# Fewer lone convolution taps on VectorE, two more whole weight tiles, and a norm's first sums written later, in a fused two-block kernel

## The chip, the cores and the metric

The kernel runs on one core of a Trainium2 chip. The metric is device time in microseconds (us) of one execution. All times below are of that core: TensorE (PE, and PEld for its weight loads), VectorE (DVE), ScalarE (ACT), GpSimd (POOL) and SyncE (SP, which issues the weight transfers).

## What is computed

Two model blocks in a row on 256 tokens of width 1024, all in fp32. The first block (retention, then latent attention) is not touched. The change lies in the first half of the second block:

```python
h = layer_norm(x) * (1.0 + sc1[:, None]) + sh1[:, None]
proj = h @ w_in[l]
a_val, a_gate, u_pool, gate_a, gate_b = jnp.split(proj, [COL_A_VAL, COL_A_GATE, COL_POOL, COL_GATE_A], axis=-1)

ya = a_val * jax.nn.sigmoid(a_gate)                     # 512 channels
ya = causal_dwconv(ya, w_dw_a[l], b_dw_a[l])            # 31 taps per channel
ya = jax.nn.silu(layer_norm(ya, ln_a_g[l], ln_a_b[l]))
ya = ya @ w_pw_a[l]

pooled = causal_multiscale_pool(u_pool)                 # windows 2, 4, 8, 16
yb = jnp.einsum("bsgc,gcd->bsgd", pooled, w_pool[l]).reshape(bsz, s, D_MODEL) * pool_scale[l]
merged = jax.nn.sigmoid(gate_a) * ya + jax.nn.sigmoid(gate_b) * yb
mix = merged @ w_out[l]
```

## The kernel before

Activations lie channels by tokens: a block is 128 channels by 256 tokens, and four blocks fill one buffer of the pool `half`, which has 14 buffers. A product in fp32 is done in one of two ways. `mm` (lines 237 to 239) takes weight and activation split into a high and a low part and makes three products; for that each weight tile of 128x1024 goes through a cast on ScalarE (`wh`, line 178) and a subtraction on VectorE (`wl`, line 179). `mm32` (line 243) takes both whole, in one fp32 instruction that runs four passes, and needs neither step. `in_tile(ps, m, parts)` picks one of the two for one tile of 128 output channels of `w_in2`.

The stretch that the change touches runs on TensorE in this order: four tiles ahead of the norm (`ahead_mm`), four tiles `[2, 6, 3, 7]` (`k_outer`), four tiles of the pool's input and two of a gate by `mm32`, then fourteen tiles of the gates by `mm` in seven pairs, with the eight small products of `w_pool` after the third pair, then `w_pw` (`half_outer`), which needs the convolution's norm `yap`.

Beside it run these steps.

- `modulate` (line 993 and on) makes the norm's output `h` per block: the high part on ScalarE (L993), the full value on VectorE (L995; kept as `hraw` in two buffers of `half` for the `mm32` tiles), the low part on VectorE (L996).
- `conv_steps` does the 31 taps for two channel blocks at a time, first half blocks 0 and 1, second half blocks 2 and 3. A step is either a **double step** (0 in `STEPS`): ScalarE scales two taps for two blocks into a fresh buffer `t` of `half` (four instructions, L1105) and VectorE adds the 128x1024 of it to the accumulator (L1106); or a **lone tap** (1): two fused multiply-adds on VectorE (L1099). The last addition of a half is L1109. `every(1.35, ...)` writes one step each 1.35 us of planned TensorE time.
- `pool(g)`, four groups: GpSimd adds shifted copies (L1165, in two buffers `lv`), VectorE finishes (L1167, L1169, L1170, buffer `pq`), and `split` makes the two parts for `w_pool` (L187, L188).
- `ln_a_first` squares the first half's result and sums both on TensorE (L1180, L1185); `ln_a` does so for the second half (L1190, L1193), and then computes the statistics, the scale, the SiLU (L1201) and its split (L187, L188), which `w_pw` waits for.

What is written where comes from a small planner in the code: `tick` counts planned TensorE time, and `after(us, fn)` and `every` write a step when its time has come. A scheduler then orders each engine's queue from that and gives each new tile a buffer; a buffer that is still held is a wait. Each engine works its queue strictly in order.

Of the kernel before, what the change touches and what calls it, by code (L numbers as in the profile page):

```python
# [14 lines left out]
AF = mybir.ActivationFunctionType  # L15
ALU = mybir.AluOpType
ADD, SUB, MUL = ALU.add, ALU.subtract, ALU.mult
# [65 lines left out]
def tile_kernel(ctx, tc, order, xT, pT, pos, vec, cst, cv, rows, wada, wts, outT):  # L83
    nc = tc.nc
    V, A, T = nc.vector, nc.scalar, nc.tensor
# [11 lines left out]
    def nm(s):  # L97
        uid[0] += 1
        return f"{s}_{uid[0]}"
# [4 lines left out]
    def bank2():  # L104
        return bank().rearrange("p (b t) -> p b t", b=2)
# [28 lines left out]
    def t2(dt=F32):  # L134
        return tp.tile([P, 2, S], dt, tag="t2", name=nm("t2"), bufs=6)
# [46 lines left out]
    def nouter(name, ms, kbs, c0=0):  # L182
        return [(name, kb * P, c0 + m * P) for m in ms for kb in kbs]
# [19 lines left out]
    def after(us, fn):  # L203
        queue.append((clk[0] + us, fn))
        queue.sort(key=lambda e: e[0])
# [79 lines left out]
    def col(name, i, n=1):  # L285
        o = VOFF[name] + i
        return vc[:, o:o + n]
# [110 lines left out]
    def bc2(t, n=2):  # L398
        return t.unsqueeze(1).to_broadcast([P, n, S])
# [25 lines left out]
    def every(us, n, step):  # L425

        def run():
            step()
            if n > 1:
                every(us, n - 1, step)  # L430
        after(us, run)
# [379 lines left out]
    for i in range(3):  # L811
        ps = bank2()
# [170 lines left out]
    def modulate(x, which, mu, nrl, pairs, pair, raw=None):  # L983

        shift = mod[:, 24 * which:24 * which + 8]
        for i in pairs:
            t = t2()
            V.tensor_sub(t, x.pair(i), bc2(mu))
            V.tensor_mul(t, t, bc2(nrl))
            for b in range(2):  # L990
                k = 2 * i + b
                m1 = ms[:, 8 * which + k:8 * which + k + 1]
                A.activation(pair[0][k], t[:, b, :], AF.Identity, bias=shift[:, k:k + 1], scale=m1)  # L993
                full = t[:, b, :] if raw is None else raw[k]
                V.tensor_scalar(full, t[:, b, :], m1, shift[:, k:k + 1], MUL, ADD)  # L995
                V.tensor_sub(pair[1][k], full, pair[0][k].bitcast(F32))  # L996


# [78 lines left out]
    def tap(i, k):  # L1077
        return apad[:, i, k:k + S], col("w_dw_a_2", 4 * k + i)


    STEPS = [0, 0, 1, 0, 0, 1, 0, 1, 0, 1, 0, 1, 0, 1, 0, 0, 1, 0]

    def conv_steps():
        for i0 in (0, 2):
            own = acc2[i0 // 2]
            for k in range(2):
                for b in range(2):
                    x, w = tap(i0 + b, k)
                    if k == 0:
                        A.activation(own[:, k, b, :], x, AF.Identity, bias=col("b_dw_a_2", i0 + b), scale=w)  # L1090
                    else:
                        A.activation(own[:, k, b, :], x, AF.Copy, scale=w)
            yield
            k = 2
            for i, alone in enumerate(STEPS):
                if alone:
                    for b in range(2):
                        x, w = tap(i0 + b, k)
                        V.scalar_tensor_tensor(own[:, 0, b, :], x, w, own[:, 0, b, :], MUL, ADD)  # L1099
                else:  # L1100
                    t = hp_.tile([P, 2, 2, S], F32, tag="half", name=nm("half"))
                    for j in range(2):
                        for b in range(2):
                            x, w = tap(i0 + b, k + j)
                            A.activation(t[:, j, b, :], x, AF.Copy, scale=w)  # L1105
                    V.tensor_add(own, own, t)  # L1106
                k += 1 if alone else 2
                if i == len(STEPS) - 1:
                    V.tensor_add(own[:, 0], own[:, 0], own[:, 1])  # L1109
                    if i0 == 2:  # L1110
                        after(0.6, ln_a)
                if i0 == 2 and i == 1:
                    ln_a_first()
                yield
            assert k == 31
# [17 lines left out]
    glu_ahead(0)  # L1133
    modulate(xt, 0, mu, nrl, range(2, 4), hp, hraw)
    glu_ahead(1)
    every(1.35, 2 + 2 * len(STEPS), conv)
    pab = k_outer("w_in2", [2, 6, 3, 7], hp)
    for i in (2, 3):
        glu(pab[i - 2], i)
# [4 lines left out]
    def in_tile(ps, m, parts):  # L1144
        seq = Seq(nouter("w_in2", [m], range(8)), parts=parts)
        for kb in range(8):
            if parts:
                mm(ps, seq.next(), rhs(hp, kb), kb == 0, kb == 7)
            else:
                mm32(ps, seq.next()[0], hraw[kb], kb == 0, kb == 7)  # L1150

    for i in range(2):
        ps = bank2()
# [66 lines left out]
    for i in range(8):  # L1220
        j = (i + 4) % 8
        ps = bank2()
        for b in range(2):
            in_tile(ps[:, b, :], 12 + 2 * j + b, i > 0)
        A.activation(sab.pair(j), ps, AF.Sigmoid)
        if i == 3:
            pool_out()
# [145 lines left out]
    for i in range(NA + 2, FB):  # L1373
        ps = bank2()
# [15 lines left out]
    ps = {(tb, o): bank()[:, :w] for tb in range(2) for o, w in chunks[tb]}  # L1390
# [27 lines left out]
    for tb in range(2):  # L1418
# [3 lines left out]
        for o, w in chunks[tb]:  # L1422
# [5 lines left out]
            t = zt[o // 512][:, o % 512:o % 512 + w]  # L1428
# [96 lines left out]
```

## Time and profile before

| | us |
|---|---|
| median of 3 runs | 862.32 (860.01 to 863.61) |
| the profiled execution | 856.09 |
| its span from first to last instruction | 854.2 |
| PE busy in the span | 826.4 (97%) |
| DVE busy | 713.1 (83%) |
| ACT busy | 551.4 (65%) |
| POOL busy | 21.6 (3%) |

The profiled execution is 1.89 us longer than its span, and 6.23 us below the median of the runs. Busy shares are averages over the whole program. Matmuls overlap each other, so the duration of one is longer than its spacing to the next; in a row "x4" with one duration, that duration is from the start of the first to the end of the last.

### The profile page before, as it was taken

The numbers are of one execution on the slowest core, as the hardware profiler recorded it, in microseconds if no ns is written. First come the engines' busy times: TensorE is split into PE (matmuls) and PEld (weight loads), VectorE is DVE, ScalarE is ACT, GpSimd is POOL, SyncE is SP. The second block draws the span as 40 slices with busy tenths as digits, with TensorE's granted clock in tenths as the row PEclk, the third lists the DMA queues.
The fourth block names the chain that finished last, engine by engine and source line by source line (L and its number), as shares of the span: only waits on it lengthen the run. The fifth ranks groups of instructions, "written<-read, shape, count | busy, mean of one in ns | idle before, by whom it ended". The sixth has DMA issues, their size and how long they took to land.

```text
span 854.2 us, 15883 instructions
## 1 busy us (share of the span) xinstructions
PE 826.4 (97%) x6178; PEld 790.3 (93%) x6178; DVE 713.1 (83%) x1276; ACT 551.4 (65%) x950; POOL 21.6 (3%) x40
## 2 busy tenths in 40 slices
PE   9999999999999999998999999989799999999995
PEld 6989999999999899998999999889699999999885
DVE  6999788988898978688864868999777888889986
ACT  7656555555675786777754767888656576666550
POOL 0000000000000000000000000310000000000001
PEclk9999999999999999999999999999899999999998
DMA  9876567788466546364345354245453355557822
GB/s 336 317 264 217 206 216 256 260 286 324 153 204 236 203 156 249 141 221 148 128 166 189 123 178 170 98 145 197 143 206 123 127 196 178 192 205 255 275 79 74
DMA packets 46635, 167.49 MB, mean 196 GB/s; under 512 B 5216, under 2 KB 5472, under 8 KB 46560
## 3 DMA queue, kind: packets, MB, share of 16 engines
q1 hardware_dynamic: 45936, 164.38, 54.2%
q0 software_dynamic: 624, 2.10, 0.8%
q8 instruction: 48, 0.79, 0.4%
q14 instruction: 27, 0.22, 0.1%
HBM read 165.41 MB, written 1.05 MB: 195 GB/s over the span
## 4 chain that ended last, share of the span: by engine, by line
PE 43%; DVE 7%; ACT 3%; issue 1%; POOL 0%; DVEq 0%; ACTq 0%
PE ps L238 13%; PE ps L239 12%; PE ps L237 12%; PE ps L243 4%; DVE half L1106 2%; ACT half L1105 1%; DVE wl L179 1%; PE ps L343 1%; DVE half L1099 1%; POOL lv L1165 0%; PE ps L365 0%; DVE half L1218 0%; PE ps L922 0%; ACT half L993 0%; DVE t L1452 0%
## 5 line engine op out<-in xcount | busy, mean ns | idle before, releaser
L237 PE MATMUL ps<-half,wh 128*128 128x256 f32 x1568 | 443.5, 284 | 7.0 <-ACT half L187 7.0
L238 PE MATMUL ps<-half,wh 128*128 128x256 f32 x1568 | 444.3, 283 | 0.8 <-DVE half L188 0.8
L239 PE MATMUL ps<-half,wl 128*128 128x256 f32 x1568 | 440.8, 281 | 2.0 <-DVE wl L179 2.0
L178 ACT CAST wh<-raw 128x1024 fp32r<-128x1024 f32 x241 | 251.2, 1049 | 165.5 <-PE ps L238 105.0
L179 DVE TENSOR_TENSOR wl<-raw,wh 128x1024 fp32r<-128x1024 f32 x241 | 292.8, 1221 | 62.7 <-ACT wh L178 60.8
L237 PEld LDWEIGHTS ps<-half,wh 128*128 128x128 f32 x1568 | 295.6, 189 | 8.1 <-ACT half L187 7.6
L239 PEld LDWEIGHTS ps<-half,wl 128*128 128x128 f32 x1568 | 296.6, 189 | 2.6 <-DVE wl L179 2.6
L238 PEld LDWEIGHTS ps<-half,wh 128*128 128x128 f32 x1568 | 296.2, 189 | 2.3 <-DVE half L188 1.4
L237 PE MATMUL ps<-wh,half 128*128 128x512 f32 (+1 forms) x202 | 72.8, 361 | 0.0
L238 PE MATMUL ps<-wl,half 128*128 128x512 f32 (+1 forms) x202 | 71.1, 352 | 0.0
L415 DVE CUSTOM_DVE_ANT_0 adach<-adach,siluc 128x1024 f32<-128x1024 f32 x48 | 58.4, 1218 | 15.2 <-DMA adach<-in_wada 14.9
L239 PE MATMUL ps<-wh,half 128*128 128x512 f32 (+1 forms) x202 | 71.0, 351 | 0.0
L243 PE MATMUL ps<-half,raw 128*128 128x260 f32 (+2 forms) x256 | 56.7, 381 | 0.0
L243 PEld LDWEIGHTS ps<-half,raw 128*128 128x128 f32 x256 | 48.4, 190 | 6.9
L237 PEld LDWEIGHTS ps<-wh,half 128*128 128x128 f32 x202 | 38.1, 188 | 5.5 <-issue 0.5
L239 PEld LDWEIGHTS ps<-wh,half 128*128 128x128 f32 x202 | 38.0, 188 | 5.6
L238 PEld LDWEIGHTS ps<-wl,half 128*128 128x128 f32 x202 | 38.1, 189 | 5.4 <-DVE wl L179 0.4
L1105 ACT ACTIVATE half<-apad,vec 128x256 f32<-128x256 f32 x88 | 37.2, 502 | 2.9 <-DVE half L1106 2.9
L187 ACT CAST half<-t 128x256 fp32r<-128x256 f32 (+1 forms) x47 | 20.6, 453 | 17.8 <-DVE t L1365 10.8
L1106 DVE TENSOR_TENSOR half<-half,half 128x1024 f32<-128x1024 f32 x22 | 27.5, 1250 | 2.5 <-ACT half L1105 1.9
L188 DVE TENSOR_TENSOR half<-t,half 128x256 fp32r<-128x256 f32 (+1 forms) x47 | 21.7, 483 | 4.5 <-ACT half L187 3.6
L1360 ACT ACTIVATE t<-ps,vec 128x256 f32<-128x256 f32 x38 | 21.0, 558 | 2.0 <-PE ps L239 1.3
(294 smaller groups left out, 925.8 us busy)
## 6 DMA issues: line engine op xcount, KB each, us to landing
raw<-in_wts SPq DMA_DIRECT2D x257, 512.0 KB, 4.1
adach<-in_wada SPq DMA_DIRECT2D x48, 512.0 KB, 4.9
half<-in_xT SPq DMA_DIRECT2D x4, 256.0 KB, 6.3
half<-in_rows POOLq DMA_DIRECT2D x2, 512.0 KB, 4.7
out<-t SPq DMA_DIRECT2D x4, 256.0 KB, 2.0
cst<-in_cst SPq DMA_DIRECT2D x1, 928.0 KB, 10.3
raw<-in_wts SPq DMA_DIRECT2D x2, 256.0 KB, 4.3
siluc<-in_cv SPq DMA_DIRECT2D x1, 512.0 KB, 8.1
```

The costliest lines, as they stand in the source:

```text
L178: A.copy(hi, raw)
L179: V.tensor_sub(lo, raw, hi.bitcast(F32))
L187: A.copy(hi, src)
L188: V.tensor_sub(lo, src, hi.bitcast(F32))
L237: T.matmul(ps, l[0], r[0], start=first, stop=False)
L238: T.matmul(ps, l[0], r[1], start=False, stop=False)
L239: T.matmul(ps, l[1], r[0], start=False, stop=last)
L243: T.matmul(ps, w, r, start=first, stop=last)
L415: V.tensor_tensor_reduce(ch, ch, sc, 1.0, 0.0, MUL, ADD, mod[:, n:n + 1])
L1105: A.activation(t[:, j, b, :], x, AF.Copy, scale=w)
L1106: V.tensor_add(own, own, t)
L1360: A.activation(t[:, b, :], ps[:, b, :], AF.Identity, bias=col("b_dw_f_2", m), scale=w[2])
```

## The change

Four edits, all in the second block's first half. (1) `modulate`: where the full value is kept as `hraw` (the first of its two uses), it is computed by ScalarE, not VectorE. (2) `STEPS`: per half three lone taps and thirteen double steps instead of seven and eleven, and the period of writing is 1.5 instead of 1.35 us. (3) The first sums of the norm are written after the fifth step of the second half, not after the second. (4) `in_tile(..., i % 4 > 0)`: the pair `i = 4` is done whole, by `mm32`, too; the pair `i = 0` already was.

```diff
                 full = t[:, b, :] if raw is None else raw[k]
-                V.tensor_scalar(full, t[:, b, :], m1, shift[:, k:k + 1], MUL, ADD)
+                if raw is None:
+                    V.tensor_scalar(full, t[:, b, :], m1, shift[:, k:k + 1], MUL, ADD)
+                else:
+                    A.activation(full, t[:, b, :], AF.Identity, bias=shift[:, k:k + 1], scale=m1)
                 V.tensor_sub(pair[1][k], full, pair[0][k].bitcast(F32))
...
-    STEPS = [0, 0, 1, 0, 0, 1, 0, 1, 0, 1, 0, 1, 0, 1, 0, 0, 1, 0]
+    STEPS = [0, 0, 0, 0, 1, 0, 0, 0, 0, 1, 0, 0, 0, 0, 1, 0]
...
-                if i0 == 2 and i == 1:
+                if i0 == 2 and i == 4:
                     ln_a_first()
...
-    every(1.35, 2 + 2 * len(STEPS), conv)
+    every(1.5, 2 + 2 * len(STEPS), conv)
...
-            in_tile(ps[:, b, :], 12 + 2 * j + b, i > 0)
+            in_tile(ps[:, b, :], 12 + 2 * j + b, i % 4 > 0)
```

The edits shift the lines behind them by three: L1099, L1105, L1106, L1109 become L1102, L1108, L1109, L1112, and L1185, L1193, L1201 become L1188, L1196, L1204. The order of the queues is the same as before up to the second block's first norm, and again from `w_pw` on. Three places show what moved between.

ScalarE around the start of the convolution's second half, before (`half<-apad` scales a tap, `wh<-raw` casts a weight tile, `half<-ps` is a gate's sigmoid, `half_6775<-half_6772` splits a pooled group):

```order
L1105 ACTIVATE half_6841<-apad,vec 128x256 x4
L1090 ACTIVATE half_6485<-apad,vec 128x256 [waits DVE_49]
L1090 ACTIVATE half_6485<-apad,vec 128x256
L1092 ACTIVATE half_6485<-apad,vec 128x256 x2
L1105 ACTIVATE half_6900<-apad,vec 128x256 x4
L1105 ACTIVATE half_6929<-apad,vec 128x256 [waits DVE_49]
L1225 ACTIVATE half_6779<-ps_6828 128x512 [waits PE_49]
L1105 ACTIVATE half_6929<-apad,vec 128x256 x3
L1180 ACTIVATE t_1233_6937<-half_6484 128x512 [waits DVE_49]
L1105 ACTIVATE half_6981<-apad,vec 128x256 [waits DVE_49]
L1105 ACTIVATE half_6981<-apad,vec 128x256 x3
L187 CAST half_6775<-half_6772 128x256
```

The same place after the change, from the last two of five weight casts and the split of the last pooled group on (the second half's first taps, L1093 and L1095, stand eleven rows above):

```order
L178 CAST wh_7079<-raw_7077 128x1024 [waits DMAHW5_49]
L178 CAST wh_7117<-raw_7115 128x1024 [waits DMAHW6_49]
L187 CAST half_6787<-half_6784 128x256 [waits DVE_49]
L1108 ACTIVATE half_6862<-apad,vec 128x256 [waits DVE_49]
L1108 ACTIVATE half_6862<-apad,vec 128x256 x3
L178 CAST wh_7227<-raw_7225 128x1024 [waits DMAHW0_49,PE_49]
L1108 ACTIVATE half_6889<-apad,vec 128x256 [waits DVE_49]
L1108 ACTIVATE half_6889<-apad,vec 128x256 x3
L178 CAST wh_7302<-raw_7300 128x1024 [waits DMAHW1_49,PE_49]
L1108 ACTIVATE half_6922<-apad,vec 128x256 [waits DVE_49]
L1108 ACTIVATE half_6922<-apad,vec 128x256 x3
```

Before, the double steps of the second half follow at once on its first taps and go on between the pooled groups. Now none stands ahead of the last pooled group's split; the first of them waits for VectorE's side of that split (it takes the buffer `pq`), and each of the next three waits for VectorE's addition of the one before.

TensorE at the last pair of gate tiles, before, from the pair's last product on:

```order
L239 MATMUL ps_7425<-half_6459,wl_7459 128x256
L1193 MATMUL ps_6935<-half_6485,ones 128x256 [waits DVE_49]
L1193 MATMUL ps_6935<-half_6485,ones 128x256
L1193 MATMUL ps_6936<-t_1290_7371,ones 128x256 [waits Activation_49]
L1193 MATMUL ps_6936<-t_1290_7371,ones 128x256
L237 MATMUL ps_7491<-half_6773,wh_7495 128x256 [waits Activation_49]
```

And after, from the pair's first product on:

```order
L237 MATMUL ps_7393<-half_6458,wh_7396 128x256 [waits PE_49,Activation_49]
L238 MATMUL ps_7393<-half_6460,wh_7396 128x256
L239 MATMUL ps_7393<-half_6458,wl_7397 128x256 [waits DVE_49]
L237 MATMUL ps_7393<-half_6458,wh_7396 128x256
L238 MATMUL ps_7393<-half_6460,wh_7396 128x256
L239 MATMUL ps_7393<-half_6458,wl_7397 128x256
L237 MATMUL ps_7393<-half_6458,wh_7396 128x256
L1196 MATMUL ps_6974<-half_6485,ones 128x256 [waits DVE_49]
```

The norm's last sums stood behind the 48 matmuls of the last pair; now they stand behind seven of them, and 41 follow.

ScalarE in the norm, before, from the square of the second half to the SiLU:

```order
L178 CAST wh_7669<-raw_7667 128x1024 [waits DMAHW3_49,DVE_49,PE_49]
L1190 ACTIVATE t_1290_7371<-half_6485 128x512 [waits DVE_49]
L389 ACTIVATE t_1291_7377<-ps_6935 128x256 [waits PE_49]
L391 ACTIVATE t_1292_7379<-ps_6935 128x256
L395 ACT_TABLE_LOAD
L395 ACTIVATE t_1294_7383<-t_1293_7381,eps_l 128x256 [waits DVE_49]
L1201 ACT_TABLE_LOAD
L1201 ACTIVATE t_1298_7391<-t_1298_7391,vec,lng 128x256 [waits DVE_49]
```

And after:

```order
L1193 ACTIVATE t_1280_7256<-half_6485 128x512 [waits DVE_49]
L389 ACTIVATE t_1281_7262<-ps_6974 128x256 [waits PE_49]
L391 ACTIVATE t_1282_7264<-ps_6974 128x256
L178 CAST wh_7534<-raw_7532 128x1024 [waits DMAHW1_49]
L395 ACT_TABLE_LOAD
L395 ACTIVATE t_1284_7268<-t_1283_7266,eps_l 128x256 [waits DVE_49]
L178 CAST wh_7570<-raw_7568 128x1024 [waits DMAHW2_49,PE_49,Activation_49]
L178 CAST wh_7637<-raw_7635 128x1024 [waits DMAHW3_49,PE_49,Activation_49]
L1204 ACT_TABLE_LOAD
L1204 ACTIVATE t_1288_7276<-t_1288_7276,vec,lng 128x256 [waits DVE_49]
```

Three weight casts that stood ahead of the norm now stand inside it, the last of them (it takes the buffer of the last gate tile's weights, and waits for TensorE to be done with them) right ahead of the SiLU; on VectorE four of their subtractions stand inside the norm in the same way.

## Rows read from the trace of the kernel before

**Rows 1.** The page's first part: busy us, share of the span, instructions.

```profile
PE 826.4 (97%) x6178; PEld 790.3 (93%) x6178; DVE 713.1 (83%) x1276; ACT 551.4 (65%) x950; POOL 21.6 (3%) x40
```

**Rows 2.** Whom PE waited for, 500 to 620: us in total, times, longest.

```profile
PE ps L237 <- ACT half L187: 5.3, 1, 5.3
PE ps L1185 <- DVE half L1109: 2.3, 1, 2.3
PE ps L239 <- DVE wl L179: 1.1, 1, 1.1
PE ps L1193 <- DVE half L1109: 0.7, 1, 0.7
```

**Rows 3.** Stretches: length, busy us of PE, PEld, DVE, ACT, POOL; clock; DMA.

```profile
580.00:590.00 10.00, 8.91 (x75) 8.71 (x74) 10.00 (x16) 10.00 (x19) 0.00 (x0) 1.00 0.49 162
590.00:600.00 10.00, 10.00 (x87) 10.00 (x86) 10.00 (x13) 6.50 (x10) 0.00 (x0) 1.00 0.72 249
600.00:610.00 10.00, 3.98 (x25) 3.19 (x23) 9.04 (x14) 6.91 (x12) 0.00 (x0) 0.87 0.68 223
...
612.00:614.00 2.00, 2.00 (x11) 2.00 (x11) 0.17 (x1) 1.99 (x3) 0.00 (x0) 0.50 0.00 0
614.00:616.00 2.00, 2.00 (x18) 2.00 (x16) 0.06 (x1) 1.14 (x2) 0.00 (x0) 0.93 0.03 8
```

**Rows 4.** Timeline of PE: start, us, instructions, [idle before and releaser].

```profile
532.83 20.88 PE L243 MATMUL ps<-half,raw 128*128 128x256 f32 x96
553.36 0.47 PE L237 MATMUL ps<-half,wh 128*128 128x256 f32 x1
...
560.50 0.28 PE L239 MATMUL ps<-half,wl 128*128 128x256 f32 x1
...
564.46 1.13 PE L1185 MATMUL ps<-half,ones 128*128 128x256 f32 x4 [2.26 <-DVE half L1109]
...
609.84 0.79 PE L237 MATMUL ps<-half,wh 128*128 128x256 f32 x2 [5.28 <-ACT half L187]
```

**Rows 5.** Timeline of ACT.

```profile
517.48 2.07 ACT L993 ACTIVATE half<-t,mod,ms 128x256 fp32r<-128x256 f32 x4 [2.14 <-DVE t L989]
520.84 0.17 ACT L1050 ACTIVATE sm<-ps 128x2 f32<-128x2 f32 x1 [1.28 <-PE ps L243]
...
535.31 4.90 ACT L1105 ACTIVATE half<-apad,vec 128x256 f32<-128x256 f32 x12
...
581.90 3.89 ACT L178 CAST wh<-raw 128x1024 fp32r<-128x1024 f32 x4
585.68 0.60 ACT L1225 ACTIVATE half<-ps 128x512 f32<-128x512 f32 x1
...
608.40 1.09 ACT L1201 ACTIVATE t<-t,vec,lng 128x256 f32<-128x256 f32 x2 [0.84 <-DVE t L1198]
```

**Rows 6.** Timeline of DVE.

```profile
564.72 2.54 DVE L1106 TENSOR_TENSOR half<-half,half 128x1024 f32<-128x1024 f32 x2
567.30 0.88 DVE L1099 SCALAR_TENSOR_TENSOR half<-apad,vec,half 128x256 f32<-128x256 f32 x2
...
576.22 2.35 DVE L179 TENSOR_TENSOR wl<-raw,wh 128x1024 fp32r<-128x1024 f32 x2
...
601.83 0.68 DVE L1109 TENSOR_TENSOR half<-half 128x512 f32<-128x512 f32 x1
602.43 2.35 DVE L179 TENSOR_TENSOR wl<-raw,wh 128x1024 fp32r<-128x1024 f32 x2
...
606.75 0.42 DVE L374 SCALAR_TENSOR_TENSOR t<-t,t 128x256 f32<-128x256 f32 x1
...
607.67 1.29 DVE L1198 TENSOR_TENSOR t<-t,t 128x512 f32<-128x512 f32 x2
```

**Rows 7.** Groups by line: duration ns min/median/max, first and last start.

```profile
L995 DVE TENSOR_SCALAR half<-t,ms,mod x8: 401/406/407, 518.0 to 526.5; 128x256 f32<-128x256 f32 x8
L1165 POOL TENSOR_TENSOR lv<-lv x6: 612/700/2642, 544.0 to 562.6; 128x256 f32<-128x256 f32 x6
```

## The prediction

> **What bounds the kernel now.** The page's first part comes first: TensorE is busy in 97% of the span [rows 1], so only its idle time and its own work can change the total. Next is the list of what TensorE waited for in the stretch that the change touches, 500 to 620 us. It has four entries [rows 2]: 5.3 us for the first split part of the convolution's norm, 2.3 and 0.7 us for the two last additions of the convolution, 1.1 us for the low part of a weight tile: 9.4 us. The table of stretches says who is late there: VectorE is busy without a gap from 580 to 600 while ScalarE is already at 65% from 590 on [rows 3]. So VectorE finishes the convolution late, at 601.83 + 0.68 [rows 6]; TensorE has done its last gate tile by 609.84 - 5.28 = 604.56 [rows 4] and has nothing left to hide the norm. Behind the long wait the granted clock is 0.50, which is 1.2 GHz, and is back near full in the slice from 614 [rows 3]: some 4.4 us at half speed, about 2.2 us lost.
>
> I sum against the profiled execution (856.09; its span 854.2 and 1.89 around it), and add the difference to the median of the runs, which lies 6.23 higher, at 862.32.
>
> **The change part by part: the engines.** Spacings, from rows with several instructions: a scaled tap on ScalarE 4.90/12 = 0.41; a weight cast 3.89/4 = 0.97 [rows 5]; a weight subtraction 2.35 - 1.2 = 1.15; a double step's addition 2.54/2 = 1.27, or 1.15 like the subtraction of the same size when it follows directly; a lone tap of two blocks 0.88, or 0.80 followed directly [rows 6]; the full value 0.41 on VectorE [rows 7] and 2.07/4 = 0.52 on ScalarE [rows 5].
> - VectorE: 8 lone taps go, -6.4 to -7.0; 4 additions come, +4.6 to +5.1; 8 full values go, -3.3; 2 subtractions go, -2.3. Net about -7.
> - ScalarE: 16 scaled taps come, +6.6; 8 full values, +4.1; 2 casts go, -1.9. Net +8.8.
> - TensorE: the whole product costs 20.88/48 = 0.435 (two records each), the split one (560.50 - 553.36)/20 = 0.357 [rows 4]; 16 are exchanged, +0.08 x 16 = +1.25, all on the path.
>
> A tap thus costs about the same on either engine (0.40 alone, 0.41 scaled), and the scaled one 0.29 of an addition on top [rows 5, 6].
>
> **The order, which decides.** If VectorE alone set the end, -7 would remove nearly all of the waits. The three places shown in the change say otherwise.
>
> (a) The first weight tiles. ScalarE now has from 517.48 on, without a gap, 16 high and full values at 0.52, 52 scalings at 0.41, two casts at 0.97, and first taps, sigmoids, copies and a table load that I estimate at 6.5: 8.3 + 21.3 + 1.9 + 6.5 = 38.0, so the first half's scalings end at 555.5. (Of the 4.1 of full values only about 1.3 falls into idle time that ScalarE had [rows 5].) VectorE follows it one step behind, and the low part of the first gate tile now stands behind the next-to-last addition of that half: ready at about 555.3. TensorE wants it at 553.6 [rows 4]. New wait: 1.7.
>
> (b) The buffer. Behind that, VectorE has the last additions of the half and six subtractions (8.6) and the small pooled pieces (2.5, an estimate), 566.4 at the earliest; these interlock with GpSimd, which has two buffers and can only go on when VectorE has read one. Its additions take 0.61 to 2.64 [rows 7]. I add 2.2 for it, a little over one stretched addition, since most rows are near the short end. The Trainium skill, "SBUF — State Buffer", section "Who interferes with whom", states that a VectorE instruction with two SBUF inputs and a GpSimd instruction that reads SBUF exclude each other, and that the one which starts first holds the shared port to its end. The longest row agrees with that, and the median of 0.70 shows that at least half of the additions escaped it; by the rows the sum below comes out, and by the rule, with all five additions of the chain stretched, 7.5 more. So the last pooled group is split at 568.6 (567 to 570), and only then has the second half its first buffer: `hraw` now keeps two buffers of `half` until the pair i = 4 is done, where before they came free at 553.36.
>
> (c) From 568.6 ScalarE needs 13 x 4 x 0.41 = 21.3 for the scalings, 5 casts 4.9, 4 sigmoids 2.4 [rows 5], and loses some 1.5 in the first four double steps, which share one buffer and so run in turn with VectorE's addition (casts fill most of the gap): 598.7. The last cast is that of the last pair's first weights; its subtraction is done 1.15 later, at 599.8. VectorE is not later than that: the second half took it 602.43 + 0.1 - 564.72 = 37.8 without a gap before [rows 6]; eight subtractions (9.2) now stand elsewhere, four lone taps go (3.2), two additions come (2.3), two small splits go (0.7), leaving 27.0 from about 570.4, 597.4 without waiting.
>
> (d) TensorE from 553.36: 88 split products at 0.357 (31.4), the norm's first sums (2.1, from [rows 4]), 16 whole products (7.0): 593.9. Waits on the way: 1.7 from (a), and about 1.4 because the pair i = 4 needs a result bank that VectorE empties only behind the third addition of the second half. So it stands before the last pair at 597.0 and waits 2.8 for the weights of 599.8. The 2.3 of the first sums goes, since they are now written where the half has long been done.
>
> (e) The tail. The norm's last sums now lie inside the last pair, so 41 matmuls run beside the statistics. But the SiLU stands behind a cast that waits for the end of that pair. From there: cast 1.05, subtraction 1.15, the last two steps of the norm on VectorE 0.45 and 0.7, and from SiLU to product 609.84 - 608.40 = 1.44 [rows 4 to 6]: 4.8, where it was 5.28. The wait that the edit was to hide is given back, 0.5 less.
>
> Sum: old waits -2.3 - 1.1 - 0.7 = -4.1; whole products +1.25; new waits +1.7 + 1.4 + 2.8 = +5.9; tail -0.5. Together +2.5. The wait of 4.8 is nearly as long as the old one, so I take the same loss of clock behind it. From `w_pw` on the order is as before and everything shifts. Edits (1), (2) and (3) cost nothing beyond these; weight transfers have their buffers several us ahead, as no wait on a DMA is in [rows 2].
>
> Forecast: 856.09 + 2.5 = 858.6 for an execution like the profiled one, and 862.32 + 2.5 = **864.8** for the median.
>
> **The rivals.**
> 1. *The new waits vanish.* If the pooled groups are done by 564 and no step waits for a buffer, TensorE is left with its work: -4.1 + 1.25 - 0.5 = -3.4, 858.9. For it: VectorE's work falls by 7, and it is the late engine in [rows 3]. Against: (c) leaves VectorE at 597.4 without a single wait, where TensorE would need the sums at 594.9 or so; half of this, -1.3 (861.0), is more likely than all. If in addition the shorter wait left the clock up, 2.2 more would go: 856.7.
> 2. *GpSimd is held off, and the half starts later; slower.* Place: (b). Five of GpSimd's additions (two of the third group, three of the fourth) lie in a chain with VectorE before the buffer comes free, at a time when VectorE runs subtractions back to back. Each takes 0.7 (median) or up to 2.64 [rows 7]; at the top the chain is 5 x 1.94 = 9.7 longer, of which 2.2 is counted. Every us goes one for one into (c), (d) and the end. It decides from 1.8 us on (a total of +4.3, 0.5%); with three of the five at the top it is +5.8 - 2.2 = +3.6, so 868.4; with all, 872.3. For it: ScalarE has no slack to catch up. Against: VectorE itself stands idle when it waits for GpSimd, which then runs at 0.6 to 0.7. This is how it would go by the rule of the Trainium skill ("SBUF — State Buffer", "Who interferes with whom") that stands in (b).
> 3. *The convolution is not held back by buffers at all* (the additions are quicker than their scalings, so one buffer is enough). Then the 1.5 in (c) goes and the rest stays: +1.0, 863.3. That is inside the forecast's range.
>
> **How the numbers follow.** Forecast (with rival 3 inside it), +0 to +4.3: 0.60. Rival 1: 0.19, of which 0.06 beyond -4.3 (its clock bonus and the scatter of a median). Rival 2 beyond +4.3: 0.21. About 0.5% (4.3 us) is what a measurement of this kernel can tell from no change. So faster by over 0.5% 0.06, within 0.73, slower 0.21. The range holds 8 in 10 from half of rival 1 with the runs' scatter of about 1.7, 859.3, to rival 2 with three stretched additions, 868.8.
>
> **What would show it.** In the profile of the changed kernel: the wait of TensorE for the first additions is gone; a wait of 1 to 2 for a weight's low part near 553; no double step of the second half on ScalarE before some 568, and the first four one addition apart; a wait of 2 to 4 for weights ahead of the last pair; a wait of 4.5 to 5 for the norm's split behind it, with a cast and a subtraction right before the SiLU, and the clock at 0.50 behind it. VectorE's busy time falls by about 7, ScalarE's rises by about 9. I am wrong if the second half starts before 565 (then rival 1) or after 571 (rival 2), or if the last wait is clearly shorter than 4.8.

## The result and the profile after

The changed kernel takes 864.45 us (median of 17 runs, 861.49 to 867.49) where the kernel before, run beside it, takes 860.01 (17 runs, 855.5 to 863.61). The ratio is 1.0058, with a 95% interval of 1.0041 to 1.0076: slower by 5.0 us (3.5 to 6.5). The profiled execution of the changed kernel took 861.49, its span 859.5; against [rows 1] its first part reads:

```profile
PE 828.1 (96%) x6162; PEld 791.9 (92%) x6162; DVE 707.5 (82%) x1254; ACT 559.2 (65%) x972; POOL 19.2 (2%) x40
```

VectorE is 5.6 us less busy, ScalarE 7.8 more (forecast: about 7 and about 9). Whom TensorE waited for from 500 to 625 (us in total, times, longest), to be held against [rows 2]:

```profile
PE ps L237 <- ACT half L187: 5.0, 1, 5.0
PE ps L239 <- DVE wl L179: 3.2, 2, 1.8
PE ps L243 <- DVE half L1221: 1.5, 1, 1.5
PE ps L237 <- ACT wh L178: 0.7, 1, 0.7
```

Four waits of 9.4 us became five of 10.4. The waits for the norm's sums are gone; there are one of 1.84 at 554.3 and one of 1.34 at 600.4 for a low part, 0.7 just before for a high part, and 1.5 at 579.2 for a result bank. The wait for the norm's split is nearly as long as it was. The stretches show what the list does not (columns as in [rows 3]; the granted clock stands after the five engines):

```profile
557.00:558.00 1.00, 1.00 (x9) 1.00 (x8) 1.00 (x2) 0.79 (x1) 0.00 (x0) 0.71 0.90 287
558.00:560.00 2.00, 2.00 (x11) 2.00 (x11) 1.55 (x4) 1.01 (x3) 1.47 (x4) 0.50 0.87 266
560.00:562.00 2.00, 2.00 (x16) 2.00 (x16) 1.71 (x2) 1.46 (x2) 1.12 (x3) 0.79 0.33 129
...
602.00:604.00 2.00, 2.00 (x8) 1.82 (x8) 2.00 (x3) 1.19 (x2) 0.00 (x0) 0.50 0.63 207
...
616.00:620.00 4.00, 4.00 (x24) 4.00 (x25) 1.25 (x4) 3.96 (x7) 0.00 (x0) 0.64 0.19 75
```

In this stretch TensorE ran at 1.2 GHz three times, behind the waits of 554, 600 and 611, where the kernel before did so once. Each took about 1.7 us of TensorE's time: 0.29 + 1.0 + 0.42 behind the first. What a drop costs in the end is another question; the filled kernels below answer it.

ScalarE's timeline where the second half of the convolution begins (start, us, instructions, idle before and releaser):

```profile
569.99 0.41 ACT L187 CAST half<-half 128x256 fp32r<-128x256 f32 x1 [3.33 <-DVE half L1173]
570.89 1.71 ACT L1108 ACTIVATE half<-apad,vec 128x256 f32<-128x256 f32 x4 [0.49 <-DVE half L188]
572.51 1.04 ACT L178 CAST wh<-raw 128x1024 fp32r<-128x1024 f32 x1
573.90 1.71 ACT L1108 ACTIVATE half<-apad,vec 128x256 f32<-128x256 f32 x4 [0.35 <-DVE half L1109]
```

As the order showed, the first double step waits for VectorE's side of the last pooled split, and the next ones come 3.0 apart, each behind VectorE's addition. The tail, on ScalarE, VectorE and TensorE:

```profile
610.71 1.05 ACT L178 CAST wh<-raw 128x1024 fp32r<-128x1024 f32 x1 [1.49 <-issue]
...
611.99 1.22 DVE L179 TENSOR_TENSOR wl<-raw,wh 128x1024 fp32r<-128x1024 f32 x1
613.13 0.42 DVE L375 SCALAR_TENSOR_TENSOR t<-t,t 128x256 f32<-128x256 f32 x1
613.58 1.29 DVE L1201 TENSOR_TENSOR t<-t,t 128x512 f32<-128x512 f32 x2
...
615.74 0.80 PE L237 MATMUL ps<-half,wh 128*128 128x256 f32 x2 [5.00 <-ACT half L187]
```

The last pair ends at 610.74. Only then run the cast that needs its weight buffer and that cast's subtraction, which stands on VectorE ahead of the norm's last two steps; then come SiLU and split. The start of `w_pw` is 5.9 later than in [rows 4]; 0.33 of it is the later start of the whole stretch (517.81 instead of 517.48), and the same 0.33 stands in every comparison of a time of the two profiles.

### The profile page after: what moved, and what is told of

The parts are those of the page before. It is cut to its first block, busy times and chain, and to the rows that moved or that the text cites. A ratio compares the mean times of both kernels' runs of the same rounds, so it can differ in the third digit from the quotient of the medians.

```text
span 859.5 us, 15843 instructions
## 1 busy us (share of the span) xinstructions
PE 828.1 (96%) x6162; PEld 791.9 (92%) x6162; DVE 707.5 (82%) x1254; ACT 559.2 (65%) x972; POOL 19.2 (2%) x40
## 4 chain that ended last, share of the span: by engine, by line
PE 40%; DVE 7%; ACT 5%; issue 2%; POOL 1%; DVEq 0%
PE ps L237 12%; PE ps L238 12%; PE ps L239 12%; PE ps L243 4%; ACT half L1108 3%; DVE half L1109 2%; DVE wl L179 2%; PE ps L343 1%; POOL lv L1168 1%; ACT half L993 0%; DVE half L1102 0%; ACT half L998 0%; PE ps L1196 0%; PE ps L922 0%; DVE t L988 0%
## 5 line engine op out<-in xcount | busy, mean ns | idle before, releaser
L243 PE MATMUL ps<-half,raw 128*128 128x256 f32 (+2 forms) x288 | 63.8, 381 | 1.5 <-DVE half L1221 1.5
L243 PEld LDWEIGHTS ps<-half,raw 128*128 128x128 f32 x288 | 54.4, 190 | 9.4 <-DVE half L1221 1.7
L1108 ACT ACTIVATE half<-apad,vec 128x256 f32<-128x256 f32 x104 | 43.2, 509 | 1.5 <-DVE half L1109 1.1
L1109 DVE TENSOR_TENSOR half<-half,half 128x1024 f32<-128x1024 f32 x26 | 32.2, 1239 | 7.1 <-ACT half L1108 5.8
```

The costliest lines, as they stand in the source:

```text
L243: T.matmul(ps, w, r, start=first, stop=last)
```

## The experiments

All twelve in one table. "Stretch" is read from each profile: from the first scaling of the norm ahead of the convolution on ScalarE (L993; 517.48 in [rows 5]) to the first scaling of the next norm (L1261; L1258 before). "Waits" is the sum of TensorE's list from 540 to 625. "Clock" is the mean granted clock of all runs, over the whole program. Whole spans of single profiles must not be compared: the stretch begins anywhere between 517.5 and 524.8, although the order ahead of it is the same in all kernels.

| kernel | ratio to before (95%) | stretch | waits | clock |
|---|---|---|---|---|
| before | 1 | 117.3 | 9.4 | 0.9906 |
| changed | 1.0058 (1.0041 to 1.0076) | 122.1 | 10.4 | 0.9898 |
| (1) undone | 1.0028 (1.0009 to 1.0047) | 119.1 | 9.8 | 0.9906 |
| (2) undone | 1.0030 (1.0007 to 1.0054) | 120.0 | 9.3 | 0.9875 |
| (3) undone | 1.0057 (1.0039 to 1.0074) | 120.9 | 10.4 | 0.9892 |
| (4) undone | 1.0023 (1.0003 to 1.0044) | 118.7 | 8.4 | 0.9893 |
| whole pair earlier | 1.0034 (1.0010 to 1.0059) | 120.1 | 7.8 | 0.9873 |
| three `lv` buffers | 1.0052 (1.0030 to 1.0075) | 121.2 | 10.2 | 0.9888 |
| (2) alone | 0.9994 (0.9973 to 1.0015) | 119.4 | 9.1 | 0.9886 |
| (4) alone | 1.0004 (0.9981 to 1.0026) | 119.9 | 8.4 | 0.9900 |
| changed, waits filled | 1.0022 (1.0002 to 1.0042) | 119.0 | 5.3 | 0.9933 |
| before, waits filled | 0.9959 (0.9939 to 0.9978) | 115.4 | 3.7 | 0.9939 |
| four pairs whole | 0.9964 (0.9944 to 0.9985) | 114.3 | 4.5 | 0.9941 |
| three pairs whole | 0.9977 (0.9952 to 1.0001) | 115.1 | 5.4 | 0.9910 |

The theories: **A**, the buffers (step (b) of the prediction): `hraw` keeps two buffers of `half`, so the second half starts late and everything behind it with it. **B**, the queues of two full engines: scalings and weight casts stand in one queue on ScalarE, and what one wins the other loses. **C**, GpSimd's two buffers (rival 2).

**Edit (4) undone.**

```diff
-            in_tile(ps[:, b, :], 12 + 2 * j + b, i % 4 > 0)
+            in_tile(ps[:, b, :], 12 + 2 * j + b, i > 0)
```

> The changed kernel with edit (4) undone: the pair i = 4 is split again, the other three edits stay. Theory A (the buffers): the kept full value is done with at about 553 as in the kernel before, its two buffers come free, and the second half's first double step starts on ScalarE at 556 to 559, not at 570.9. The long stretch with idle VectorE (2.83 of 5 us busy at 570 to 575) goes. TensorE gains 1.25 on the products, and the waits ahead of the last pair (0.7 + 1.3) with the clock loss behind them (1.7) go: span 852 to 856, against 859.5 of the changed kernel. The wait at 554 (1.8) stays, with its clock loss. Theory B (the work of the engines: ScalarE got 8.8 us more, VectorE 7 less): ScalarE gets 1.9 and VectorE 2.3 us of weight work back, TensorE gains 1.25: 858 to 861, and the wait ahead of the last pair is 2 or longer.

The second half does start early; its stretch begins 4.24 later than that of the changed kernel, so 561.46 is 557.2 there, 13.7 ahead of 570.89 (ScalarE's timeline, then TensorE's waits):

```profile
561.46 3.29 ACT L1108 ACTIVATE half<-apad,vec 128x256 f32<-128x256 f32 x8
...
PE ps L239 <- DVE wl L179: 5.1, 3, 2.5
PE ps L237 <- ACT wh L178: 2.4, 1, 2.4
PE ps L237 <- ACT half L187: 0.9, 1, 0.9
```

The wait for the norm falls from 5.0 to 0.9, but two of about 2.5 for weights appear, between 567 and 574, with the scalings ahead of the casts, and the clock is at 0.50 behind them. The start is A's, the time is B's: 13.7 us of earlier start are worth 0.0035, or 3.0 us (the two intervals just overlap), and of these 1.25 are the whole products that go with the edit.

**The whole pair earlier (i = 1 instead of i = 4).**

```diff
-            in_tile(ps[:, b, :], 12 + 2 * j + b, i % 4 > 0)
+            in_tile(ps[:, b, :], 12 + 2 * j + b, i > 1)
```

> The changed kernel with the same two whole tiles more, but as the second pair (i = 1) instead of the fifth (i = 4): the work of every engine is the same. Theory A (the buffers): the kept full value is done with some 7 us after the first pair, at about 560, so the second half starts on ScalarE at 556 to 561; and TensorE wants the first split weights only at 560, so the wait of 1.8 at 554 and the clock loss of 1.7 behind it go too. With the waits ahead of the last pair and their clock loss gone as well (2.0 + 1.7): at least 7 less than 859.5, span 849 to 852.5. Theory B (work of the engines): nothing but the wait at 554 goes (its 1.8 and 1.7 come back later, since ScalarE is what ends last): 858 to 860.

TensorE's waits, then two of its stretches (length, busy, clock, DMA):

```profile
PE ps L237 <- ACT wh L178: 5.2, 2, 2.7
PE ps L239 <- DVE wl L179: 2.6, 2, 2.0
...
586.00:588.00 2.00, 2.00 (x11) 0.50 0.73 252
...
598.00:600.00 2.00, 2.00 (x11) 0.50 0.78 252
```

The wait at 554 and the one for the norm are both gone, as A expected, and the second half's first double step comes 8.5 earlier (569.37, 562.4 in the changed kernel's time; A had 556 to 561). In their place TensorE waits 7.8 us for weights between 581 and 595, and runs at half speed behind both pairs of waits. A falls as the account of the time: the same work in a better place loses elsewhere most of what it wins here, 2.1 us are left (0.0024, within the scatter of the two intervals). The loss shows in the clock too. Its mean, 0.9873, is 0.0033 under that of the kernel before, which over the whole run is 2.8 us (an estimate, and an upper bound, since part of the low clock lies inside waits); the kernel is 2.9 slower. For the kernel with (2) undone, below, the same estimate is 2.7, and it is 2.6 slower.

**Three buffers for GpSimd.**

```diff
-        t = sp.tile([P, 16 + S], F32, tag="lv", name=nm("lv"), bufs=2)
+        t = sp.tile([P, 16 + S], F32, tag="lv", name=nm("lv"), bufs=3)
```

> The changed kernel with three buffers instead of two for GpSimd's shifted sums; otherwise the same. Theory C (the chain of GpSimd and VectorE through two buffers sets the time of the last pooled split, 570.0, and so the start of the second half): GpSimd no longer waits for VectorE, the last pooled split moves to 566 to 568, the second half's first double step with it, TensorE's waits ahead of the last pair get 2 to 3 shorter: span 855.5 to 858. Theory A (what holds the second half is the wait for a buffer as such, and VectorE's own queue behind the first half is as long as before): the split moves by less than 1, span 858.5 to 860.5.

```profile
572.14 1.71 ACT L1108 ACTIVATE half<-apad,vec 128x256 f32<-128x256 f32 x4 [1.51 <-DVE half L188]
```

Less the 1.72 by which its stretch begins later, the first double step starts at 570.4, where the changed kernel has 570.9, and the ratio is 1.0052. C falls as the account of the time, though the buffer does free GpSimd: its last addition ends at 560.2 (558.5 in the changed kernel's time, 566.9 there).

```profile
558.68 1.55 POOL L1168 TENSOR_TENSOR lv<-lv 128x256 f32<-128x256 f32 x1
...
568.34 1.99 ACT L178 CAST wh<-raw 128x1024 fp32r<-128x1024 f32 x2
...
569.41 2.36 DVE L179 TENSOR_TENSOR wl<-raw,wh 128x1024 fp32r<-128x1024 f32 x2 [1.09 <-ACT wh L178]
...
PE ps L239 <- DVE wl L179: 5.1, 2, 3.7
```

The split then stands in the queues of the two other engines, behind two casts on ScalarE and two subtractions on VectorE. And the pooled pieces that VectorE now does sooner stand ahead of the first low part: that wait is 3.7 instead of 1.84. The bank and the last high part are not waited for here, so that the sum, 10.2, is as before.

**Edit (1) undone.**

```diff
-                if raw is None:
-                    V.tensor_scalar(full, t[:, b, :], m1, shift[:, k:k + 1], MUL, ADD)
-                else:
-                    A.activation(full, t[:, b, :], AF.Identity, bias=shift[:, k:k + 1], scale=m1)
+                V.tensor_scalar(full, t[:, b, :], m1, shift[:, k:k + 1], MUL, ADD)
```

> The changed kernel with edit (1) undone: the kept full value is computed on VectorE again. My sum: the first half's scalings end some 2 to 3 earlier on ScalarE, the low part of the first gate tile is ready before TensorE wants it, and the wait of 1.8 at 554 goes; with it the granted clock stays at 1.00 from 557 to 561, which saves 1.7 more there. The second half still starts behind the last pooled split (568 to 570), so that part of it comes back as a longer wait ahead of the last pair: span 857 to 859. If the drop of the clock at 557 is not due to that wait but to the whole products in front of it, it stays where it is, and the span is 858.5 to 861.

```profile
PE ps L237 <- ACT half L187: 4.8, 1, 4.8
PE ps L243 <- DVE half L1218: 2.3, 1, 2.3
PE ps L239 <- DVE wl L179: 2.0, 3, 1.4
```

The wait of 1.84 at the first weight tile shrinks to 0.4 (at 557.4), the clock stays at 1.00 from 550 to 610, and 0.8 comes back as a longer wait for the bank. The ratio is 0.0030 lower, 2.6 us (the intervals just overlap). That is the size of my sum for this place, but the gain is made elsewhere. The pair i = 4 waits for its bank in both kernels, so what TensorE saved ahead of it cannot pass; the pair starts at 582.25, 579.1 in the changed kernel's time and 1.6 before 580.71, because the second half too starts 1.6 earlier (572.43, 569.3), and the low part of the last pair is 1.6 earlier as well. In this profile there is also no drop of the clock behind the wait of 600.

**Edit (2) undone**, and then **edit (2) alone** on the kernel before (the same lines the other way round).

```diff
-    STEPS = [0, 0, 0, 0, 1, 0, 0, 0, 0, 1, 0, 0, 0, 0, 1, 0]
+    STEPS = [0, 0, 1, 0, 0, 1, 0, 1, 0, 1, 0, 1, 0, 1, 0, 0, 1, 0]
...
-    every(1.5, 2 + 2 * len(STEPS), conv)
+    every(1.35, 2 + 2 * len(STEPS), conv)
```

> The changed kernel with edit (2) undone (seven lone taps per half again, written every 1.35); edits (1), (3), (4) stay. After the runs with edit (4) undone and with the whole pair moved, where the second half started 9 and 12 us earlier and TensorE then waited for weight casts behind the scalings instead, theory B says: ScalarE's work ahead of the weight casts is what is too much, and the 6.6 of scaled taps are most of it. Then this kernel has no wait ahead of the last pair, is late only by VectorE at the norm as the kernel before, and the ratio is 0.999 to 1.002. Theory A (the hold of the second half by two kept buffers): the hold is untouched by this edit, VectorE has 2 more to do behind it, so the ratio is that of the changed kernel or worse, 1.005 to 1.009.

> The kernel before with edit (2) alone: three lone taps per half and the period 1.5. Theory B (ScalarE's 6.6 more of scalings stand ahead of the casts of the weights that TensorE wants next): waits for weights at 562 to 566 and at 585 to 590, none over 1 for the norm, 1.003 to 1.007. Theory of VectorE's late end (its 2 us less bring the norm 2 earlier, ScalarE has room from 590 on): 0.997 to 0.9995.

TensorE's waits without the taps, and (below the dots) with nothing but them:

```profile
PE ps L237 <- ACT half L187: 4.8, 1, 4.8
PE ps L243 <- DVE half L1221: 4.1, 1, 4.1
...
PE ps L239 <- DVE wl L179: 4.1, 3, 3.0
PE ps L237 <- ACT wh L178: 4.1, 2, 2.2
PE ps L237 <- ACT half L187: 0.9, 1, 0.9
```

Undone, the ratio (1.0030) lies between what the two theories gave: the waits for weights are gone as B said, but VectorE is late with the bank of the whole pair, 4.1 instead of 1.5. Alone, the taps make the trade of B: 8.2 us of waits for weights where the kernel before has 1.1, and 0.9 for the norm where it has 5.3. But the sum is 9.1 against 9.4, and the ratio 0.9994: B's price, 1.003 to 1.007, falls. The other theory's 0.997 to 0.9995 holds the number, but not by its way: what the norm gave back went to the weights.

**Edit (3) undone.**

```diff
-                if i0 == 2 and i == 4:
+                if i0 == 2 and i == 1:
```

> The changed kernel with edit (3) undone: the first sums of the norm are written after the second step of the second half again. My sum: the wait of 2.3 for them in the kernel before was time that TensorE would have spent waiting at the end anyway, where VectorE's end decides; so the place of these sums is worth nothing as long as something else ends later: ratio within 0.001 of the changed kernel's 1.0058 (1.0045 to 1.007), first sums without a wait or with one that shortens the later ones by as much. If the edit by itself gave the 2.3, this kernel is 2 to 2.5 slower than the changed one: 1.008 to 1.009.

The list of waits is that of the changed kernel, entry for entry, without one for the first sums, and the ratio is 1.0057. In the changed kernel the place of these sums is worth nothing, and it was not this edit that took the 2.3 away. Edit (3) alone on the kernel before was not run, nor edit (1) alone.

**Edit (4) alone.** On the kernel before:

```diff
-            in_tile(ps[:, b, :], 12 + 2 * j + b, i > 0)
+            in_tile(ps[:, b, :], 12 + 2 * j + b, i % 4 > 0)
```

> The kernel before with edit (4) alone: the fifth pair whole. Two casts and two subtractions less, TensorE +1.25, two buffers kept until 580. Theory of VectorE's late end: the norm comes 2.3 earlier, ratio 0.997 to 0.9995, and TensorE's wait for the norm is 1.75 or less longer than... its own 1.25 taken off the old 9.4. Theory A (the buffers): the second half starts late, the norm with it: 1.001 to 1.004, with the wait for the norm still 5 or longer.

```profile
PE ps L237 <- ACT half L187: 4.8, 1, 4.8
PE ps L243 <- DVE half L1218: 1.8, 1, 1.8
PE ps L1185 <- DVE half L1109: 1.4, 1, 1.4
```

The ratio, 1.0004, lies between the two forecasts and settles nothing. The list shows what (4) brings by itself: the wait for a bank ahead of the whole pair appears, and the norm is still 4.8 late, as the buffers would have it.

**The clock by itself: waits filled with products that nobody reads.** Ahead of `w_pw`, 14 in the changed kernel, 13 in the one before:

```diff
+    fp = bank()[:, :S]
+    for n in range(14):
+        T.matmul(fp, ones, up[n % 4][:, 16:], start=True, stop=True)
     half_outer("w_pw", yap, fin_pw, 4)
```

> The changed kernel with 14 products more on TensorE that nobody reads (the pool's input times ones, 0.435 each): three stand in the wait for the last pair's low part (1.34), eleven (4.8) in the wait for the norm (5.0). They add no other work, and the two waits end when they ended before. Clock theory: what I had left out of the sum is that TensorE comes out of such waits at half speed; with the engine busy in them the granted clock stays at 1.00 there and 1.7 us are saved for each drop that goes, two of the three: 1.7 to 3.4 us, ratio 1.002 to 1.004 where the changed kernel has 1.0058. The drop behind the wait at 554, which is not filled, may stay. If the low clock costs nothing on the path (what follows waits for other engines anyway): 1.005 to 1.0065.

> The kernel before with 13 such products, two in the short wait at 602 (0.7) and eleven (4.8) in the wait for the norm (5.3). Clock theory: the 4.4 us at half speed behind that wait go, 2.2 us: ratio 0.9965 to 0.9985. If the low clock costs nothing on the path: 0.9995 to 1.001. Both numbers together say how much of the difference between the two kernels is clock: with both filled it is the sum without the clock, +1.0 of waits and +1.25 of whole products, 0.0025 to 0.0035 between them.

The changed kernel filled: its waits, its last two stretches, and the fill itself on TensorE's timeline (two records for each product):

```profile
PE ps L243 <- DVE half L1221: 2.5, 1, 2.5
PE ps L239 <- DVE wl L179: 2.1, 2, 1.8
PE ps L237 <- ACT wh L178: 0.7, 1, 0.7
...
600.00:610.00 10.00, 9.29 (x64) 1.00 0.45 156
610.00:620.00 10.00, 9.95 (x66) 1.00 0.61 213
...
610.83 4.91 PE L1242 MATMUL ps<-upad,ones 128*128 128x256 f32 x22
```

And the kernel before filled:

```profile
600.00:610.00 10.00, 9.70 (x60) 1.00 0.84 256
610.00:620.00 10.00, 9.90 (x75) 1.00 0.14 47
...
606.99 4.91 PE L1239 MATMUL ps<-upad,ones 128*128 128x256 f32 x22
```

Behind the filled waits the clock is 1.00, and both kernels get faster, by 0.0036 (3.1 us) and by 0.0041 (3.5 us). The products themselves bring no start forward: in the kernel before, `w_pw` starts where it did, at 611.90 less the 2.16 by which this stretch begins later, 609.7 (609.84 in [rows 4]). In the changed kernel it starts at 615.74 less 1.74, 614.0 instead of 615.74, as the drop behind the wait of 600 is gone. That the low clock costs time is shown. But it costs both kernels about the same; with the waits filled they lie 0.0063 apart, 0.0058 without. The clock is not the main thing that separates them (with intervals of 0.002 to either side, a part of up to some 2 us is not excluded).

Not every drop costs. The filled changed kernel shows none behind the first wait, which is not filled, and yet its pair i = 4 starts at 582.45, 580.71 in the changed kernel's time, where the changed kernel with its drop has 580.71 too. The bank was the later limit, and it was waited for 2.5 instead of 1.5.

**Versions with more whole pairs.** Four pairs whole, five lone taps per half, first sums after the fifth step, without edit (1); and three pairs whole with edit (1).

```diff
-    STEPS = [0, 0, 1, 0, 0, 1, 0, 1, 0, 1, 0, 1, 0, 1, 0, 0, 1, 0]
+    STEPS = [0, 0, 0, 1, 0, 0, 1, 0, 0, 1, 0, 0, 1, 0, 0, 1, 0]
...
-                if i0 == 2 and i == 1:
+                if i0 == 2 and i == 4:
...
-            in_tile(ps[:, b, :], 12 + 2 * j + b, i > 0)
+            in_tile(ps[:, b, :], 12 + 2 * j + b, i > 3)
```

> A version made from what the runs showed: the kernel before with the first four pairs of gate tiles whole (six weight tiles fewer to split), five lone taps per half, first sums of the norm after the fifth step. TensorE: 48 products at 0.08 more, +3.7. ScalarE and VectorE each lose six steps of a weight (5.8 and 6.9), and TensorE wants no split weight before 575, when the first half of the convolution and the pooled groups are done. Theory B (the weight steps stand in the queues of two engines that are both full): waits between 550 and 610 fall from 9.4 to under 3, with no drop of the clock there: ratio 0.991 to 0.997. Theory A: the kept full value holds two buffers until 575, so the second half starts late as in the changed kernel and the norm is late: ratio 1.002 to 1.008.

> As the version before it, but with three pairs whole (four weight tiles fewer to split, TensorE +2.5) and with the kept full value on ScalarE, edit (1). Theory B: waits under 4 between 550 and 610, at most one drop of the clock: ratio 0.992 to 0.998. Theory A: the two buffers are held until some 567, the second half starts then, and the norm is late as in the changed kernel: 1.001 to 1.006.

The first of them, its first part and its waits:

```profile
PE 827.4 (97%) x6130; PEld 788.0 (92%) x6130; DVE 705.2 (83%) x1264; ACT 548.5 (64%) x952; POOL 21.1 (2%) x40
...
PE ps L1193 <- DVE half L1109: 2.2, 1, 2.2
PE ps L239 <- DVE wl L179: 1.4, 1, 1.4
PE ps L237 <- ACT half L187: 0.9, 1, 0.9
```

Both are under both kernels in the median, the first clearly (0.9964, 3.1 us under the kernel before), the second not clear of the kernel before (up to 1.0001). Both lie in B's range of ratios, with waits of 4.5 and 5.4 where B had under 3 and under 4. In the first, both engines have less to do, TensorE wants no split weight until the pooled groups are done, and the clock is 1.00 through the whole stretch. Its mean clock, 0.9941, is 0.0035 above that of the kernel before, an estimate of 3.0 us: nearly the whole gain, and about what filling the waits alone gave. Which of the three edits in it does this was not separated. The hold of A is there too (the first double step of the second half comes at 567.73, 563.5 in the changed kernel's time) and does no harm. The fill was not tried on top of it.

## Why the prediction was right, and where it was not

The forecast of the median, 864.8, is 0.35 from the measured 864.45, and its range holds it. That closeness is luck. I had added +2.5 to a median of 862.32 from three runs; with more runs the kernel before is at 860.01, 2.3 lower, and the change is +5.0 (3.5 to 6.5), twice the forecast. As a change it lies above the +4.3 at which I had let the forecast's case end and rival 2 begin; the path, though, is that of the forecast, as the points below show. In the forecast's own terms the two profiles give +1.25 of whole products and +1.0 of waits, +2.25 against +2.5. The mechanism held; what was short is what the sum left out.

- **The waits removed (-4.1)** are gone, except that the 1.1 for a low part has a successor. I gave the 2.3 of the first sums to edit (3); with (3) undone they are not waited for either. What took the wait away is the rest of the change, and the step, as an effect of that edit, was wrong.
- **Step (a)**, the first low part: 1.84 measured, 1.7 forecast, and undoing (1) removes most of it. Right as a wait; as a term of its own it is worth nothing while the bank is the later limit, since without it the wait for the bank is longer by as much.
- **Step (b)**, the last pooled split: 569.99 instead of 568.6, and the second half's first scaling at 570.89, just inside the 565 to 571 that I had set. In GpSimd's chain two of the five additions took 1.70 and 1.55, some 1.9 over the usual 0.7; I had counted 2.2. The rest is that VectorE does two weight subtractions (2.35 from 567.28) before the last small pieces. The Trainium skill ("SBUF — State Buffer", "Who interferes with whom") says that a VectorE instruction with two SBUF inputs and a GpSimd instruction that reads SBUF contend, and that the order of issue decides which one is blocked. The trace agrees, on both sides: the addition of 562.80 began with a subtraction and took 1.70; the one of 564.62 began 0.08 ahead of the next subtraction and took 0.63, and it was the subtraction that took 1.63 instead of 1.22. That all five additions would be stretched was my reading of the rule, and too simple.

```profile
562.80 1.70 POOL L1168 TENSOR_TENSOR lv<-lv 128x256 f32<-128x256 f32 x1
...
564.62 0.63 POOL L1168 TENSOR_TENSOR lv<-lv 128x256 f32<-128x256 f32 x1
...
562.80 1.22 DVE L179 TENSOR_TENSOR wl<-raw,wh 128x1024 fp32r<-128x1024 f32 x1
...
564.70 1.63 DVE L179 TENSOR_TENSOR wl<-raw,wh 128x1024 fp32r<-128x1024 f32 x1
```

- **What (b) is worth** was right for a small shift and wrong for a large one. I wrote that every us goes one for one into (c), (d) and the end. The second half started 2.3 later than in my sum, and TensorE came to the last pair 2.2 later; with (1) undone both are 1.6 earlier. But with (4) undone 13.7 us of earlier start gave 3.0, 1.25 of them by the products. Behind the late start stands a second limit: ScalarE cannot do scalings and casts earlier, only in another order.
- **Steps (c), (d)**: the last low part ends at 601.66 instead of 599.8; TensorE reaches the pair at 599.2 instead of 597.0 and waits 2.0 instead of 2.8; the bank costs 1.5 (1.4 forecast) in this execution, 2.5 in the filled one. These times follow the second half's start, which is 2.3 late.
- **Step (e)**: 5.0 measured, 4.8 forecast, with the cast and the subtraction of the rows above. The old wait was given back almost whole, as forecast.
- **The clock** was the term that I set to zero difference. In the two profiles it is +2.9 (three drops of 1.7 against 2.2 once), which together with +1.0 of waits and +1.25 of whole products would make 5.2 of the 4.8 by which the stretches differ. That account is tempting, and other runs speak against it: the first of the three drops costs nothing in the end (the pair i = 4 starts at 580.71 with and without it), the mean clock of all runs differs by 0.0008 only (an estimate of 0.7 us), and filling takes about as much from one kernel as from the other. Both profiles were cheap executions, 3.9 under the median of the kernel before and 3.0 under that of the changed one.
- **What then makes +5.0?** The filled profiles, at full clock through the whole stretch, differ by 119.0 - 115.4 = 3.6: 1.25 of whole products, 1.6 of waits (5.3 - 3.7), 0.4 for the one product more that fills waits, and 0.3 that I cannot name. With 0.7 of clock that is 4.3 of the 5.0, and the remaining 0.7 is below the half-width of the interval (1.5). This is an account of single profiles, not a proof: the profile of the filled changed kernel is 1.5 under its median (860.21 to 861.69), and the two filled kernels differ by 0.0063, 5.4 us, where their profiles show 3.6. What makes the difference beyond these terms stays open.

Of the rivals, the first (waits vanish) needed the pooled groups done by 564; they were not. The second (GpSimd) did not happen: two of its five additions were stretched, by 1.9 in all, less than the 2.2 that the forecast counts; and a third buffer, which let GpSimd finish 8 us earlier, left the ratio where it was. The measured +5.0 lies in the band of this rival by its size alone. The third, no hold-back by buffers, was valued at 1.5 less; the two kernels that free them early came out 3.0 and 2.1 under the changed one, though by another way than that: their waits went to the weights. Two figures of the working were off and change nothing: half of rival 1 is -1.7 and not -1.3, and rival 2 with three stretched additions is 868.4, where the upper bound has 868.8.

The edits do not add up. Undoing (1), (2) or (4) each takes back 0.0028 to 0.0035 of 0.0058, and (2) and (4) alone cost nothing that can be measured. That each fills the slack that another one needs fits this, but is not shown by itself.

## What to carry to other kernels

When two helper engines are both full, a late start that is cured is paid again as another wait. Price a step one for one only up to the next limit behind it: here a shift of 1.6 went through, and of 13.7 only 3.0 were left. Taking work away from both of them, even at a cost on the bounding engine (whole fp32 products instead of split ones, where split weights are wanted first), gained what shifting work between them did not; by the mean clock most of that gain came by the clock, which was not tested apart. Where TensorE must wait some us, products that nobody reads, placed in the wait, kept its clock up and gained 3 us here, with no other cost seen. And before a forecast is added to a median, the median needs more than three runs: that one was 2.3 too high.

## What the runs showed of the hardware

The clock fell behind waits far shorter than the 5.3 us of [rows 4]: behind 1.84 us in the changed kernel's profile, and behind 1.83 at 581 with (4) alone (0.83 from 580 to 590). It does not always: in the filled one the same wait, 1.84 us at 556.0, has no drop behind it, nor has the one of 2.3 at 562 in the kernel before. Drops also fall where no edit changed anything: the granted clock is 0.91 from 180 to 200 and from 300 to 320 in the profile of the kernel with the whole pair earlier, and 0.91 from 280 to 300 in both filled ones. So a single profile says little about what the clock costs; the mean granted clock of many runs does (0.9873 for the kernel with two pairs of waits for weights, 0.9941 for the one with four pairs whole).
